# Entry of the up-projection: another order of the token halves Y, earlier places for split weights, and a written order for the stretch

## The chip, the cores and the metric

The kernel runs on one core of one Trainium2 chip. Its metric is the time in microseconds (us) of one execution on the device, as a median of three runs. TensorE (PE) does the matmuls, ScalarE (ACT) the activations, casts and copies, VectorE (DVE) most of the elementwise sums, GpSimd (POOL) a few products and the DMAs that accumulate; SyncE (SP) issues the other DMAs of this stretch. Each engine works through its own queue in order and waits on semaphores for the others.

## The reference, cut to what matters

One layer of an encoder in float32, with 512 tokens of 1024 channels. A mixing block (a gated recurrence beside attention) is followed by a feed-forward block. The change concerns the passage from the first to the second:

```python
h = rms_norm(x, ffn_norm_pre[layer])
up = jnp.einsum("bsd,df->bsf", h, w_up[layer])              # 1024 -> 6144
up = causal_dwconv(up, conv_f_w[layer], conv_f_b[layer])    # 3 taps over the tokens
gate, val = jnp.split(up, 2, axis=-1)
ffn_out = jnp.einsum("bsf,fd->bsd", jax.nn.gelu(gate) * val, w_down[layer])
x = x + rms_norm(ffn_out, ffn_norm_post[layer])
```

## The kernel before

**The split.** Every large product keeps float32 accuracy by splitting both sides into a high part (a cast) and a low part (what the cast lost). It takes three matmuls: high by high, high by low, low by high. The activations of the up-projection are `h2h` and `h2l`. The weights come as 48 tiles of 128 output channels, `up0` to `up47`. Tile `j` (gate) and tile `j + 24` (value) make pair `j`.

**Two kinds of tiles.** Pairs 0 to 2 are plain: their six tiles (`first` in the code: 0, 24, 1, 25, 2, 26) are split whole, and each is multiplied for token half X (`first_half`, tokens 0 to 255) and later for token half Y (tokens 256 to 511). One half is a `project_half` of 24 matmuls, 16 with the high weight and then 8 with the low one. Pairs 3 to 23 (class `Pair`) are done with a Strassen-like scheme, seven products in place of eight, each a `product` of 12 matmuls. The scheme needs:

- sums of activations over quarters, `sh` (ACT casts) and `sl`, made by `token_sums` from `hf`, one step for token tile 2 and one for token tile 3;
- plain pieces of raw weight tiles, `mh` (an ACT cast, `plain_high`) and `ml`: `plain_low` has ACT write the negative (L360), and POOL then issues a DMA that adds the raw weights to it (L361). For pair 3's first piece, DVE makes `ml`;
- sums of weights `t` (DVE, `sums`), with `th` (ACT cast, `sums_hi`) and `tl` (DVE, `sums_lo`). `th` and `tl` are taken from the same rotating buffers (tags `wh` and `wl`, four each) as the split weights of plain tiles 1, 25, 2 and 26;
- copies `x` of finished PSUM pieces (ACT, `keep`, L420) that DVE adds to others (`add`, L432).

**After a tile.** The convolution of a tile starts with one ACT instruction (`tap`, L1283) and goes on with two DVE instructions (`taps`, L1289), which read PSUM. For a pair there follow a gelu on ACT (L1293), a product `yf` on POOL (L1297) and a store to `yd`. For the plain pairs these steps are `first_tap`, `first_taps` and `first_glu`.

**What sets the order.** Up to the Y halves a scheduler arranges the instructions, from the code order and its own costs. From `man2` on (`manual_schedule`) each engine's queue has the order of the code. There `p` and `n` are pairs 3 and 4, the entry is written out by hand, and then the function `period` repeats for each pair: product 5 of the current pair, its sums, product 6, product 4 of the pair before, product 3, products 1 and 2 of the next pair, and product 7. In the entry PE goes through the Y halves and pair 3's products 1, 2 and 5, and then through the periods. `up_epilogue` says at which step of a period the tap, taps, gelu and GLU product of the pair before are done; in the first period, which has no pair before, its step 3 does the GLU of plain pairs 1 and 2.

**Where things lie.** The tiles `u` and `xn` of the norm (`mix_norm`) are in pool `norm`, as `hf` is. The pools `strassen` and `strassen1`, which hold `mh` and `ml`, are opened after the block `mix` is closed, that is behind the Y halves.

Of the kernel before, what the change touches and what calls it, by code (L numbers as in the profile page):

```python
# [63 lines left out]
def kernel(  # L64
# [162 lines left out]
    def project_half(dst, unit, ah, al, c):  # L227
        wh, wl = unit
        for k in range(KD):
            pe.matmul(dst[:, c], wh[:, k], ah[:, k, c], start=k == 0, stop=False)  # L230
            pe.matmul(dst[:, c], wh[:, k], al[:, k, c], start=False, stop=False)  # L231
        for k in range(KD):
            pe.matmul(dst[:, c], wl[:, k], ah[:, k, c], start=False, stop=k == KD - 1)
# [106 lines left out]
    class Pair:  # L340
# [36 lines left out]
                self.w[3] = quarter(h, l, A)  # L377

        def plain(self, i):
            self.plain_low(i)  # L380
            self.plain_high(i)

        def sums(self, i):
            r0, r1 = self.r
# [762 lines left out]
    def up_pair(j):  # L1147
        return Pair(ups, j, (f"up{j}", f"up{j + JF}"))

    turned = {}  # L1150
    with ExitStack() as mix:
# [2 lines left out]
        special["up0"] = special[f"up{JF}"] = wfpool  # L1154
        hf = npool.tile([P, KD, S], F32, name="hf", bufs=1)
        gb = [npool.tile([P, D], F32, name=f"gain{i}", bufs=1) for i in range(2)]
        for i in range(2):
            nc.sync.dma_start(gb[i], gains[i + 1 : i + 2, :].partition_broadcast(P))

        def mix_norm(t, acc):  # L1160
            u = npool.tile([P, D], F32, tag="u", name=f"u{t}")
            xn = npool.tile([P, D], F32, tag="xn", name=f"xn2_{t}")
            s2 = small.tile([P, 2], F32, tag="s2", name=f"s2_mix{t}")
            for i, c in enumerate(HALVES):
                act.activation(out=xn[:, c], in_=acc[t][i], func=AF.Square, accum_out=s2[:, i : i + 1])
                dve.tensor_tensor(out=u[:, c], in0=acc[t][i], in1=gb[0][:, c], op=ALU.mult)
            yield
            ss = small.tile([P, 1], F32, tag="ss", name=f"ss_mix{t}")
            dve.tensor_tensor(out=ss, in0=s2[:, 0:1], in1=s2[:, 1:2], op=ALU.add)
            rs = rstd_of(ss, f"mix{t}")  # L1170
            if t > 1:
                yield
            s3 = small.tile([P, 2], F32, tag="s2", name=f"s2_f{t}")
            for i, c in enumerate(HALVES):
                dve.scalar_tensor_tensor(out=x2t[:, t, c], in0=u[:, c], scalar=rs, in1=x2t[:, t, c],
                                         op0=ALU.mult, op1=ALU.add)
                act.activation(out=xn[:, c], in_=x2t[:, t, c], func=AF.Square, accum_out=s3[:, i : i + 1])
            yield
            ss = small.tile([P, 1], F32, tag="ss", name=f"ss_f{t}")
            dve.tensor_tensor(out=ss, in0=s3[:, 0:1], in1=s3[:, 1:2], op=ALU.add)  # L1180
            rs = rstd_of(ss, f"f{t}")
            for c in HALVES:
                dve.scalar_tensor_tensor(out=xn[:, c], in0=x2t[:, t, c], scalar=rs, in1=gb[1][:, c],
                                         op0=ALU.mult, op1=ALU.mult)
            yield
            turned[t] = to_channels(xn, t, h2h, h2l, hf, "f")
# [29 lines left out]
        def token_sums(t):  # L1216

            c1, c2 = (slice(P * (t - 2 + d), P * (t - 1 + d)) for d in (0, 2))
            f11, f12 = hf[:, :KH, c1], hf[:, KH:, c1]
            f21, f22 = hf[:, :KH, c2], hf[:, KH:, c2]  # L1220
            dve.tensor_tensor(out=f22, in0=f21, in1=f22, op=ALU.add)
            dve.tensor_tensor(out=f21, in0=f11, in1=f21, op=ALU.subtract)
            dve.tensor_tensor(out=f11, in0=f22, in1=f11, op=ALU.subtract)
            dve.tensor_tensor(out=f12, in0=f12, in1=f11, op=ALU.subtract)
            yield
            for i, f in enumerate((f22, f11, f21, f12)):
                act.copy(sh[i][:, :, c1], f)
                dve.tensor_tensor(out=sl[i][:, :, c1], in0=f, in1=sh[i][:, :, c1].bitcast(F32), op=ALU.subtract)
# [3 lines left out]
        def first_half(e, ready_only=False):  # L1232
            first.append((bank(f"up{e}"), unit(f"up{e}", 0)))
            project_half(*first[-1], h2h, h2l, X)
# [21 lines left out]
        s2 = token_sums(2)  # L1256
        next(s2)
        first_half(2 + JF)
        with ExitStack() as later:
            for i in turned[NT - 1]:  # L1260
                later.enter_context(tc.issue_after(i.ins))
            pairs[NU].sums(0)
            pairs[NU].sums(1)
            pairs[NU + 1] = up_pair(NU + 1)
            next(s2, None)
            for _ in token_sums(3):
                pass
        for ps, u in first:
            project_half(ps, u, h2h, h2l, Y)

    ypool = fstk.enter_context(tc.tile_pool(name="ff", bufs=3, reuse_waits="tile"))
    ydram = ctx.enter_context(tc.tile_pool(name="ffd", bufs=1, space=bass.MemoryType.DRAM))
    yd = [ydram.tile([P, 2, S], F32, name=f"yd{j}") for j in range(JF // 2)]
    upool = ustk.enter_context(tc.tile_pool(name="up", bufs=3, reuse_waits="tile"))
    offset(ustk, 32, "right")
    st1pool = ustk.enter_context(tc.tile_pool(name="strassen1", bufs=2, side="right", reuse_waits="tile"))
    offset(ustk, 416, "right")
    ups.stpools = [ustk.enter_context(tc.tile_pool(name="strassen", bufs=2, side="right", reuse_waits="tile")), st1pool]
    ups.kpool = upool

    def tap(e, ps, tag):
# [18 lines left out]
    def up_epilogue(b, which, step):  # L1300
        if which == "a" and step > 1 and not b:
            if step == 3:
                first_glu(1)
                first_glu(2)
        elif b and step == 0:
            e, ps, tag = (b.j, b.a, "cg") if which == "a" else (b.j + JF, b.c, "cv")
            b.u = getattr(b, "u", {})
            b.u[which] = tap(e, ps, tag)
        elif b and step == 1:
            e, ps = (b.j, b.a) if which == "a" else (b.j + JF, b.c)  # L1310
            taps(e, ps, b.u[which])
        elif b and step == 2:
            gelu(b.u["a"])
        elif b:
            glu(b.j, b.u["a"], b.u["c"])
# [3 lines left out]
    def first_tap(j):  # L1319
        fe[j] = [tap(e, first[2 * j + i][0], t) for i, (e, t) in enumerate(((j, "cg"), (j + JF, "cv")))]  # L1320

    def first_taps(j):
        for i, e in enumerate((j, j + JF)):
            taps(e, first[2 * j + i][0], fe[j][i])

    def first_glu(j):
        gelu(fe[j][0])
        glu(j, *fe[j])
# [1 line left out]
    man2 = ExitStack()  # L1330
    man2.enter_context(tc.manual_schedule())
    p, n = pairs[NU], pairs[NU + 1]
    p.sums_hi(0)
    p.sums_lo(0)
    p.sums_hi(1)
    p.sums_lo(1)
    p.plain_high(0)
    p.plain(1)
    n.sums(0)
    first_tap(0)  # L1340
    n.sums(1)
    first_taps(0)
    first_tap(1)
    n.plain(0)
    p.p12()
    p.keep(2, p.a[:, Y])
    p.add(p.a[:, X], p.a[:, X], 2)
    pairs[NU + 2] = up_pair(NU + 2)
    p.p5()
    n.sums_hi(0)  # L1350
    n.sums_lo(0)
    p.keep(1, p.c[:, X])
    first_taps(1)
    first_tap(2)
    n.sums_hi(1)
    n.sums_lo(1)
    first_glu(0)
    first_taps(2)
    PRODUCTS = (1, 4, 5, 6, 7, 3, 2)
    WQ = {1: (0, 0), 2: (1, 0), 3: (1, 1), 4: 3, 5: 0, 6: 1, 7: 2}  # L1360
    STEPS = [(n, m) for n in PRODUCTS for m in range(NS)]
# [337 lines left out]
```

## Time and profile before

| what | value |
| --- | --- |
| median of three runs | 922.22 us (921.89 to 922.26) |
| profiled execution | 919.4 us |
| its span, first to last instruction | 917.6 us |
| granted clock of PE | 0.999 |
| PE busy | 905.7 us (99%) |
| DVE busy | 723.1 us (79%) |
| ACT busy | 597.9 us (65%) |
| POOL busy | 216.5 us (24%) |

The profiled execution takes 1.8 us beside its span. Times inside it count from the start of the span. The six X halves end near 576 us, the Y halves run to 592 us, pair 3's first product follows, and the periods then take some 9.6 us each. In a row of the timeline stand the start, the length, the engine, the line, the operation, what it writes and reads, a count, and in square brackets how long the engine idled just before and what released it. Tile names have no number there. In the tables of order below they have one: `up_6736` is one tile, `_3` in `ml_3_6708` is the pair.

### The profile page before, as it was taken

To read this page: it belongs to the slowest core of one execution; us is meant where nothing else is said; L and a number is where in the kernel's file an instruction comes from. 1 tells how busy PE (TensorE), PEld (TensorE's weight loads), DVE (VectorE), ACT (ScalarE), POOL (GpSimd) and SP (SyncE) were. 2 spreads that over 40 slices of the span, in tenths; PEclk is the share of its full clock that TensorE was granted. 3 is DMA by queue.
4 is the path that set the end of the run, shared out by engine and by line. 5 is a ranking of instruction groups with operands and counts; after the bars stand their busy time and mean duration, and the time that the engine had idled before them with its cause. 6 is when DMAs were issued, how large, how long until landed. Compare 5 with 4: busy or idle time off the path is not lost.

```text
span 917.6 us, 15844 instructions
## 1 busy us (share of the span) xinstructions
PE 905.7 (99%) x5870; PEld 803.5 (88%) x5870; DVE 723.1 (79%) x1190; ACT 597.9 (65%) x1034; POOL 216.5 (24%) x279
## 2 busy tenths in 40 slices
PE   9999999999999999999999999999999999999997
PEld 7988888878899987888888889999999999978886
DVE  5966369638867657888868588899999999889897
ACT  7555495433467655676654487698888888676664
POOL 4134345444111112112104100042323223100000
PEclk9999999999999999999999999999999999999999
DMA  7777589989877776334415654289988988799764
GB/s 283 242 206 210 163 214 246 273 221 188 196 184 187 183 272 231 114 131 170 156 64 166 207 185 143 58 215 219 224 228 213 241 203 210 225 370 328 238 202 147
DMA packets 71760, 187.07 MB, mean 204 GB/s; under 512 B 7233, under 2 KB 27761, under 8 KB 71298
## 3 DMA queue, kind: packets, MB, share of 16 engines
q1 hardware_dynamic: 47648, 127.72, 41.6%
q0 software_dynamic: 23888, 58.20, 29.3%
q8 instruction: 46, 0.75, 0.3%
q14 instruction: 32, 0.26, 0.1%
q10 hardware_dynamic: 146, 0.14, 0.0%
HBM read 150.69 MB, written 35.73 MB: 203 GB/s over the span
## 4 chain that ended last, share of the span: by engine, by line
PE 94%; DMA 2%; DVE 2%; issue 1%; ACT 1%; POOL 0%; SPq 0%; DVEq 0%; ACTq 0%; POOLq 0%
PE up L416 7%; PE up L414 7%; PE up L413 7%; PE dn L1411 4%; PE dn L1409 4%; PE dn L1410 4%; PE pa L218 2%; PE ga L220 2%; PE ga L218 2%; PE pa L219 2%; PE pa L220 2%; PE ga L219 2%; PE q L218 2%; PE k L218 2%; PE pb L218 2%; PE wo L1141 2%
## 5 line engine op out<-in xcount | busy, mean ns | idle before, releaser
L1289 DVE SCALAR_TENSOR_TENSOR u<-up,cpt,u 128x511 f32<-128x511 f32 x96 | 71.2, 745 | 2.6 <-ACT u L1283 0.9
L361 POOL DMA_DIRECT2D ml<-raw_up x41 | 35.3, 862 | 153.6 <-ACT ml L360 78.8
L1409 PE MATMUL dn<-wh_dn,ah 128*128 128x512 f32 (+1 forms) x180 | 67.6, 376 | 0.7 <-ACT ah L1377 0.7
L1411 PE MATMUL dn<-wh_dn,al 128*128 128x512 f32 (+1 forms) x180 | 67.7, 376 | 0.0
L1410 PE MATMUL dn<-wl_dn,ah 128*128 128x512 f32 (+1 forms) x180 | 67.6, 375 | 0.0
L413 PE MATMUL up<-sh,th 128*128 128x256 f32 x252 | 60.3, 276 | 0.4 <-DVE up L432 0.4
L414 PE MATMUL up<-sl,th 128*128 128x256 f32 x252 | 60.2, 276 | 0.0
L175 DVE TENSOR_TENSOR wl_dn<-raw_dn,wh_dn 128x1024 fp32r<-128x1024 f32 x42 | 51.5, 1227 | 8.6 <-ACT wh_dn L172 8.4
L172 ACT CAST wh_dn<-raw_dn 128x1024 fp32r<-128x1024 f32 x42 | 44.1, 1050 | 18.2 <-issue 11.5
L325 DVE TENSOR_TENSOR tl<-t,th 128x1024 fp32r<-128x1024 f32 x42 | 51.1, 1216 | 2.8 <-ACT th L395 2.8
L1283 ACT ACTIVATE u<-up,cpt 128x512 f32<-128x512 f32 x48 | 37.0, 779 | 20.4 <-PE up L416 11.1
L413 PEld LDWEIGHTS up<-sh,th 128*128 128x128 f32 x252 | 47.3, 188 | 0.6 <-DVE up L432 0.6
L395 ACT CAST th<-t 128x1024 fp32r<-128x1024 f32 x42 | 43.9, 1044 | 5.5 <-PE up L231 2.1
L414 PEld LDWEIGHTS up<-sl,th 128*128 128x128 f32 x252 | 47.3, 188 | 0.0
L1297 POOL TENSOR_TENSOR yf<-u,u 128x512 f32<-128x512 f32 x23 | 30.6, 1333 | 63.5 <-issue 43.9
L413 PE MATMUL up<-h2h,mh 128*128 128x256 f32 x168 | 40.2, 276 | 0.0
L414 PE MATMUL up<-h2l,mh 128*128 128x256 f32 x168 | 40.2, 276 | 0.0
L1409 PEld LDWEIGHTS dn<-wh_dn,ah 128*128 128x128 f32 x180 | 33.9, 188 | 7.1 <-ACT ah L1377 1.1
L1411 PEld LDWEIGHTS dn<-wh_dn,al 128*128 128x128 f32 x180 | 33.9, 188 | 7.0 <-DVE al L325 0.8
L1410 PEld LDWEIGHTS dn<-wl_dn,ah 128*128 128x128 f32 x180 | 33.9, 188 | 6.0
L416 PE MATMUL up<-sh,tl 128*128 128x256 f32 x252 | 38.8, 276 | 0.0
L1000 ACT ACTIVATE P<-P,mx 128x384 f32<-128x384 f32 (+2 forms) x64 | 35.2, 552 | 3.7 <-DVE mx L995 2.8
(719 smaller groups left out, 3219.3 us busy)
## 6 DMA issues: line engine op xcount, KB each, us to landing
raw_up<-in_w_up_dram SPq DMA_DIRECT2D x48, 512.0 KB, 5.2
td<-in_w_down_dram POOLq DMA_DIRECT2D x36, 512.0 KB, 6.7
raw_dn<-td SPq DMA_DIRECT2D x24, 512.0 KB, 5.0
B<-cnd POOLq DMA_DIRECT2D x16, 640.0 KB, 5.5
ml<-raw_up POOLq DMA_DIRECT2D x20, 512.0 KB, 5.8
raw_dn<-in_w_down_dram SPq DMA_DIRECT2D x18, 512.0 KB, 4.5
raw_wo<-in_w_out_dram SPq DMA_DIRECT2D x16, 512.0 KB, 4.3
td<-td POOLq DMA_DIRECT2D x12, 512.0 KB, 13.2
```

The source lines that it names most:

```text
L172: act.copy(self.wh, self.raw)
L175: engine.tensor_tensor(out=self.wl, in0=self.raw, in1=self.wh.bitcast(F32), op=ALU.subtract)
L218: pe.matmul(dst, ah, bh, start=first, stop=False)
L325: dve.tensor_tensor(out=out, in0=a, in1=b, op=ALU.subtract)
L395: act.copy(self.th[i], self.t[i])
L413: pe.matmul(dst, wh[:, k], ah[:, k], start=first and k == 0, stop=False, skip_group_check=True)
L414: pe.matmul(dst, wh[:, k], al[:, k], start=False, stop=False, skip_group_check=True)
L416: pe.matmul(dst, wl[:, k], ah[:, k], start=False, stop=k == KH - 1, skip_group_check=True)
L1289: dve.scalar_tensor_tensor(out=c[:, s:], in0=ps[:, : S - s], scalar=col(C_CFW + 3 * e + j), in1=c[:, s:], op0=ALU.mult, op1=ALU.add)
L1409: pe.matmul(d[:, x], ah[:, k, tok], wh[:, k, x], start=first, stop=False, skip_group_check=True)
L1410: pe.matmul(d[:, x], ah[:, k, tok], wl[:, k, x], start=False, stop=False, skip_group_check=True)
L1411: pe.matmul(d[:, x], al[:, k, tok], wh[:, k, x], start=False, stop=last, skip_group_check=True)
```

## The change

It does four things.

1. `plain(i)` does nothing if the piece is there already.
2. `u` and `xn` get a pool of their own, `norm2`, which is closed after the last X half. The pools for `mh` and `ml` are opened there, so these can be written during the Y halves.
3. The stretch behind `p.sums` is put under `manual_schedule`. Pair 3's plain pieces are made at its start, the first step of `token_sums(3)` follows, the Y halves go in the order 1, 25, 2, 26, 0, 24, and the first `th` and `tl` of pair 3 and the rest of `token_sums(3)` come behind them in the code.
4. The written entry of `man2` is put in another order. Pair 4's weight sums and pieces come earlier; plain pairs 1 and 2 are tapped before plain pair 0. `first_taps` can do one tile of a pair. In step 3 of the first period stand now the taps of tile 24 and the GLU of plain pairs 2 and 0.

```diff
         def plain(self, i):
-            self.plain_low(i)
-            self.plain_high(i)
+            if i not in self.ml:
+                self.plain_low(i)
+                self.plain_high(i)
...
+        nstk = ExitStack()
+        n2pool = nstk.enter_context(tc.tile_pool(name="norm2", bufs=2, reuse_waits="tile"))
...
-            u = npool.tile([P, D], F32, tag="u", name=f"u{t}")
-            xn = npool.tile([P, D], F32, tag="xn", name=f"xn2_{t}")
+            u = n2pool.tile([P, D], F32, tag="u", name=f"u{t}")
+            xn = n2pool.tile([P, D], F32, tag="xn", name=f"xn2_{t}")
...
         first_half(2 + JF)
+        nstk.close()
+        offset(ustk, 32, "right")
+        st1pool = ustk.enter_context(tc.tile_pool(name="strassen1", bufs=2, side="right", reuse_waits="tile"))
+        offset(ustk, 416, "right")
+        ups.stpools = [ustk.enter_context(tc.tile_pool(name="strassen", bufs=2, side="right", reuse_waits="tile")), st1pool]
         with ExitStack() as later:
...
             pairs[NU + 1] = up_pair(NU + 1)
+        with tc.manual_schedule():
             next(s2, None)
-            for _ in token_sums(3):
-                pass
-        for ps, u in first:
-            project_half(ps, u, h2h, h2l, Y)
+            p.plain_high(0)
+            p.plain(1)
+            s3 = token_sums(3)
+            next(s3)
+            for ps, u in first[2:] + first[:2]:
+                project_half(ps, u, h2h, h2l, Y)
+            p.sums_hi(0)
+            p.sums_lo(0)
+            next(s3, None)
...
             if step == 3:
-                first_glu(1)
+                first_taps(0, 1)
                 first_glu(2)
+                first_glu(0)
...
-    def first_taps(j):
-        for i, e in enumerate((j, j + JF)):
-            taps(e, first[2 * j + i][0], fe[j][i])
+    def first_taps(j, *which):
+        for i in which or (0, 1):
+            taps(j + JF * i, first[2 * j + i][0], fe[j][i])
...
-    p.sums_hi(0)
-    p.sums_lo(0)
     p.sums_hi(1)
     p.sums_lo(1)
-    p.plain_high(0)
-    p.plain(1)
+    n.plain(0)
     n.sums(0)
-    first_tap(0)
     n.sums(1)
-    first_taps(0)
     first_tap(1)
-    n.plain(0)
+    first_taps(1)
+    first_tap(2)
     p.p12()
+    n.sums_hi(0)
+    n.sums_hi(1)
+    n.plain(1)
     p.keep(2, p.a[:, Y])
     p.add(p.a[:, X], p.a[:, X], 2)
     pairs[NU + 2] = up_pair(NU + 2)
     p.p5()
-    n.sums_hi(0)
     n.sums_lo(0)
     p.keep(1, p.c[:, X])
-    first_taps(1)
-    first_tap(2)
-    n.sums_hi(1)
     n.sums_lo(1)
-    first_glu(0)
+    first_glu(1)
+    first_tap(0)
     first_taps(2)
+    first_taps(0, 0)
```

Three places show what this does to the queues. The first is ACT's, from the first copy of pair 3 (`x_3`) to the first copy of pair 4 (`x_4`). `u_` are tiles of the convolution, `up_6222` and `up_6247` are plain tiles 0 and 24, `up_6430` and `up_6459` plain tiles 2 and 26. Before:

```order
L420 COPY x_3_6785<-up_6768 128x256
L1283 ACTIVATE u_6791<-up_6430,cpt 128x512
L1283 ACTIVATE u_6793<-up_6459,cpt 128x512
L395 CAST th_4_6795<-t_4_6720 128x1024
L1293 ACT_TABLE_LOAD
L1293 ACTIVATE u_6716<-u_6716 128x512
L420 COPY x_3_6819<-up_6736 128x256
L360 ACTIVATE ml_4_6821<-raw_up_6491 128x512
L369 CAST mh_4_6824<-raw_up_6491 128x512
L360 ACTIVATE ml_5_6826<-raw_up_6764 128x1024
L369 CAST mh_5_6841<-raw_up_6764 128x1024
L420 COPY x_4_6868<-up_6843 128x256
```

And after, where `up_6225` and `up_6250` are plain tiles 0 and 24, and the gelu is that of plain pair 1:

```order
L421 COPY x_3_6799<-up_6784 128x256
L1304 ACT_TABLE_LOAD
L1304 ACTIVATE u_6731<-u_6731 128x512
L1294 ACTIVATE u_6807<-up_6225,cpt 128x512
L1294 ACTIVATE u_6809<-up_6250,cpt 128x512
L421 COPY x_3_6829<-up_6743 128x256
L360 ACTIVATE ml_5_6831<-raw_up_6780 128x1024
L369 CAST mh_5_6846<-raw_up_6780 128x1024
L421 COPY x_4_6873<-up_6848 128x256
```

The second `th` of pair 4 and the `ml` and `mh` of its second tile have gone from between the copies; they stand ahead of pair 3's first copy.

The second place is DVE's queue from pair 3's first add to the steps `t` of pair 5. Before (the two taps `L1289` of each tile read `up_6300` and `up_6371`, plain tiles 1 and 25, then `up_6430` and `up_6459`):

```order
L325 TENSOR_TENSOR tl_4_6783<-t_4_6713,th_4_6781 128x1024
L1289 SCALAR_TENSOR_TENSOR u_6727<-up_6300,cpt,u_6727 128x511
L1289 SCALAR_TENSOR_TENSOR u_6727<-up_6300,cpt,u_6727 128x510
L1289 SCALAR_TENSOR_TENSOR u_6729<-up_6371,cpt,u_6729 128x511
L1289 SCALAR_TENSOR_TENSOR u_6729<-up_6371,cpt,u_6729 128x510
L325 TENSOR_TENSOR tl_4_6797<-t_4_6720,th_4_6795 128x1024
L1289 SCALAR_TENSOR_TENSOR u_6791<-up_6430,cpt,u_6791 128x511
L1289 SCALAR_TENSOR_TENSOR u_6791<-up_6430,cpt,u_6791 128x510
L1289 SCALAR_TENSOR_TENSOR u_6793<-up_6459,cpt,u_6793 128x511
L1289 SCALAR_TENSOR_TENSOR u_6793<-up_6459,cpt,u_6793 128x510
L432 TENSOR_TENSOR up_6843<-up_6843,x_4_6868 128x256
L432 TENSOR_TENSOR up_6768<-up_6736,x_3_6785 128x256
```

And after (`up_6433` and `up_6462` are plain tiles 2 and 26):

```order
L325 TENSOR_TENSOR tl_4_6801<-t_4_6728,th_4_6770 128x1024
L1300 SCALAR_TENSOR_TENSOR u_6739<-up_6433,cpt,u_6739 128x511
L1300 SCALAR_TENSOR_TENSOR u_6739<-up_6433,cpt,u_6739 128x510
L1300 SCALAR_TENSOR_TENSOR u_6741<-up_6462,cpt,u_6741 128x511
L1300 SCALAR_TENSOR_TENSOR u_6741<-up_6462,cpt,u_6741 128x510
L1300 SCALAR_TENSOR_TENSOR u_6807<-up_6225,cpt,u_6807 128x511
L1300 SCALAR_TENSOR_TENSOR u_6807<-up_6225,cpt,u_6807 128x510
L433 TENSOR_TENSOR up_6848<-up_6848,x_4_6873 128x256
L1300 SCALAR_TENSOR_TENSOR u_6809<-up_6250,cpt,u_6809 128x511
L1300 SCALAR_TENSOR_TENSOR u_6809<-up_6250,cpt,u_6809 128x510
L433 TENSOR_TENSOR up_6784<-up_6743,x_3_6799 128x256
L433 TENSOR_TENSOR up_6784<-up_6784,x_3_6829 128x256
```

The other `tl` of pair 4 stands just ahead of this piece. Between pair 3's add and pair 4's add there are two `tl` and six taps where there were two `tl` and eight taps, and two taps now follow pair 4's add.

The third place is POOL's queue, from the DMA for pair 3's second tile on. Before, with the GLU products `yf` of plain pairs 0, 1 and 2 in this order:

```order
L361 DMA ml_3_6708<-raw_up_6427 128x512
L361 DMA ml_4_6731<-raw_up_6490 128x1024
L1297 TENSOR_TENSOR yf_6800<-u_6716,u_6718 128x512
L361 DMA ml_4_6821<-raw_up_6491 128x512
L361 DMA ml_5_6826<-raw_up_6764 128x1024
L1297 TENSOR_TENSOR yf_6876<-u_6727,u_6729 128x512
L1297 TENSOR_TENSOR yf_6880<-u_6791,u_6793 128x512
L361 DMA ml_5_6910<-raw_up_6765 128x512
```

And after, with the GLU products of plain pairs 1, 2 and 0:

```order
L361 DMA ml_3_6526<-raw_up_6430 128x512
L361 DMA ml_4_6720<-raw_up_6508 128x1024
L361 DMA ml_4_6772<-raw_up_6509 128x512
L1308 TENSOR_TENSOR yf_6804<-u_6731,u_6733 128x512
L361 DMA ml_5_6831<-raw_up_6780 128x1024
L1308 TENSOR_TENSOR yf_6883<-u_6739,u_6741 128x512
L1308 TENSOR_TENSOR yf_6887<-u_6807,u_6809 128x512
L361 DMA ml_5_6917<-raw_up_6781 128x512
```

The DMA for pair 4's second tile has moved ahead of the first GLU product; the rest keeps its sequence, with other pairs in the three products.

More of the change, by code (lines that the diff above doesn't have):

```diff
@@ L1261 @@
                 later.enter_context(tc.issue_after(i.ins))
[L1262 to L1263 removed]
+            p = pairs[NU]
+            p.sums(0)
+            p.sums(1)
             pairs[NU + 1] = up_pair(NU + 1)
+        with tc.manual_schedule():
             next(s2, None)
[L1266 to L1269 removed]
+            p.plain_high(0)
[7 more added lines that the diff above has]
+            next(s3, None)
     ypool = fstk.enter_context(tc.tile_pool(name="ff", bufs=3, reuse_waits="tile"))
@@ L1274 @@
     upool = ustk.enter_context(tc.tile_pool(name="up", bufs=3, reuse_waits="tile"))
[L1275 to L1278, printed above, removed]
     ups.kpool = upool
```

## The prediction

> **What bounds the kernel now.** I read first the busy times on the page, then TensorE's waits, then, around the one pair of waits that the change can touch, the timelines of four engines.
>
> ```profile
> PE 905.7 (99%) x5870; PEld 803.5 (88%) x5870; DVE 723.1 (79%) x1190; ACT 597.9 (65%) x1034; POOL 216.5 (24%) x279
> ...
> PE up L416 <- DMA ml<-raw_up: 0.9, 1, 0.9
> ...
> PE dn L1409 <- ACT ah L1377: 0.7, 1, 0.7
> ...
> PE up L413 <- DVE up L432: 0.4, 1, 0.4
> ```
>
> TensorE (PE) is busy 99% of the span. It sets the time, and the change leaves its instructions as they are: only a stall of PE can be won or made. The list of its waits (engine, line, waited for: total, times, longest) has two in the up-projection, one for an `ml` of a pair and one for a sum of VectorE (DVE). The rest lie before and after the stretch that is edited; one of them, 0.7 in the down-projection, is shown. What the two cost is read from PE's timeline, since a wait also holds the pipelined matmuls behind it (columns: start, length, operation; an L416 row is the last third of one `product`):
>
> ```profile
> 595.40 0.62 PE L416 MATMUL up<-sh,tl 128*128 128x256 f32 x4
> ...
> 600.88 0.62 PE L416 MATMUL up<-h2h,ml 128*128 128x256 f32 x4
> 602.24 0.62 PE L416 MATMUL up<-sh,tl 128*128 128x256 f32 x4
> 603.60 0.62 PE L416 MATMUL up<-sh,tl 128*128 128x256 f32 x4
> ...
> 605.67 0.62 PE L416 MATMUL up<-sh,tl 128*128 128x256 f32 x4
> ...
> 608.42 0.64 PE L416 MATMUL up<-sh,ml 128*128 128x256 f32 x4
> 610.87 0.74 PE L416 MATMUL up<-h2h,ml 128*128 128x256 f32 x4 [0.89 <-DMA ml<-raw_up]
> 612.35 0.62 PE L416 MATMUL up<-h2h,ml 128*128 128x256 f32 x4
> ...
> 616.43 0.62 PE L416 MATMUL up<-sh,tl 128*128 128x256 f32 x4
> ```
>
> An undisturbed product takes 1.36 us (602.24 to 603.60). Stall 1: the last third of pair 4's product 6 starts at 605.67, 2.07 after the one before, so 0.71 is lost; it waits for pair 4's first add. Stall 2: from 608.42 over pair 5's product 1 to its product 2 at 612.35 are 3.93 for two products of 2.72, so 1.21 is lost; it waits for the `ml` of pair 5's first raw tile. Together 1.92 us, and nothing else in the stretch is PE's loss. The first places to look are the engines that came late:
>
> ```profile
> 594.69 0.37 ACT L420 COPY x<-up 128x256 f32<-128x256 f32 x1 [1.46 <-PE up L416]
> ...
> 596.05 0.37 ACT L420 COPY x<-up 128x256 f32<-128x256 f32 x1
> 596.32 1.45 ACT L1283 ACTIVATE u<-up,cpt 128x512 f32<-128x512 f32 x2
> 597.66 1.05 ACT L395 CAST th<-t 128x1024 fp32r<-128x1024 f32 x1
> ...
> 600.82 0.63 ACT L360 ACTIVATE ml<-raw_up 128x512 fp32r<-128x512 f32 x1
> ...
> 601.86 1.06 ACT L360 ACTIVATE ml<-raw_up 128x1024 fp32r<-128x1024 f32 x1
> ...
> 603.76 0.37 ACT L420 COPY x<-up 128x256 f32<-128x256 f32 x1
> 596.05 1.23 DVE L325 TENSOR_TENSOR tl<-t,th 128x1024 fp32r<-128x1024 f32 x1 [0.52 <-ACT th L395]
> ...
> 601.21 2.97 DVE L1289 SCALAR_TENSOR_TENSOR u<-up,cpt,u 128x511 f32<-128x511 f32 x4
> 604.16 1.23 DVE L432 TENSOR_TENSOR up<-up,x 128x256 f32<-128x256 f32 x3
> ```
>
> Stall 1 has two causes that end together. ScalarE (ACT) makes the copy `x` at 603.76 to 604.13, though the product that it copies was out at 601.50 (600.88 and 0.62). DVE ends its four taps at 604.18 and only then adds. Either alone, taken away, would leave the other. Stall 2 is read from the chain of waits (start, length, what):
>
> ```profile
> 600.75 1.03 POOL yf L1297
> ...
> 603.22 7.61 DMA ml<-raw_up
> ```
>
> GpSimd (POOL) issues pair 5's accumulating DMA at 603.22, behind ACT's `ml` of 601.86, a GLU product and the DMA of pair 4's second tile; it lands 7.61 later.
>
> **The change, part by part.** *Order of the Y halves and of the entry.* The casts `th` need slots that the split weights of plain tiles 1, 25, 2 and 26 hold until their Y halves' high matmuls end:
>
> ```profile
> 577.27 1.07 PE L233 MATMUL up<-h2h,wl_up 128*128 128x256 f32 x8
> ...
> 585.43 1.07 PE L233 MATMUL up<-h2h,wl_up 128*128 128x256 f32 x8
> 578.69 1.29 ACT L1227 CAST sh<-hf 128x512 fp32r<-128x512 f32 x2 [4.03 <-DVE hf L1221]
> 580.67 0.62 ACT L1227 CAST sh<-hf 128x512 fp32r<-128x512 f32 x1 [0.69 <-DVE hf L1223]
> 581.88 0.62 ACT L1227 CAST sh<-hf 128x512 fp32r<-128x512 f32 x1 [0.58 <-DVE hf L1224]
> 582.90 1.05 ACT L395 CAST th<-t 128x1024 fp32r<-128x1024 f32 x1 [0.41 <-PE up L231]
> 585.62 1.05 ACT L395 CAST th<-t 128x1024 fp32r<-128x1024 f32 x1 [1.67 <-PE up L231]
> ```
>
> The first two rows are the low thirds of the first and the fourth Y half, two of four rows that stand 2.72 apart, each starting as its high part ends. Tiles 1 and 25 stand third and fourth now, with 582.71 and 585.43, and the two casts of pair 3 start right behind. First and second in the order, they are free at 577.27 and 579.99, 5.44 earlier, and the two slots for pair 4 at 582.71 and 585.43. PE does the same matmuls: 0 in itself. What the earlier casts free is room on ACT and DVE ahead of 594.69, where ACT now idles 1.46, so pair 4's two `th` and its second tile's `ml` and `mh` can stand ahead of the first copy.
>
> *ACT between the two copies.* Between 596.05 and 603.76 it loses the second `th` (1.05) and the `ml` and `mh` of 512 columns (600.82 to 601.86, 1.04): 2.09. The two taps that were there are replaced by those of plain pair 0, the gelu by that of pair 1: equal. The copy moves to 601.67, just after its product (601.50), and ends at 602.04.
>
> *DVE between the two adds.* It keeps two `tl`, and six of eight taps stand ahead of pair 4's add. Two taps of 0.74 (2.97 over 4) go behind, and the 0.52 wait for `th` goes with the earlier casts: 604.16 less 1.48 and 0.52 is 602.16. The add, a third of 1.23, ends at 602.57; PE wants it when product 5's last four matmuls are issued (a third of 1.36 after 603.60), at 604.05. Stall 1 goes with 1.5 us to spare: −0.71.
>
> *POOL and the DMA.* Pair 5's `ml` on ACT starts 2.09 earlier, at 599.77, and ends at 600.83. Only one GLU product stands ahead of the DMA on POOL. Its gelu is no longer behind two taps (596.32 to 597.66, 1.34) and the `th` (1.05), so from 600.75 it moves up by 2.39 to 598.36 and ends by 600.07, with the 1.71 of its row below. Issue at 600.87. PE, without stall 1, wants it at 608.42 and 1.36 less 0.71, at 609.07. With its own 7.61 it lands at 608.48.
>
> ```profile
> DMA to landing us min/median/max: 4.6/6.0/8.5
> 600.75 1.71 POOL L1297 TENSOR_TENSOR yf<-u,u 128x512 f32<-128x512 f32 x1 [7.27 <-ACT u L1293]
> ...
> 604.74 3.00 POOL L1297 TENSOR_TENSOR yf<-u,u 128x512 f32<-128x512 f32 x2 [0.59 <-ACT u L1293]
> 605.30 1.29 DVE L325 TENSOR_TENSOR t<-raw_up,raw_up 128x512 f32<-128x512 f32 x1
> 606.51 1.78 DVE L325 TENSOR_TENSOR t<-raw_up 128x512 f32<-128x512 f32 x1
> 608.21 1.52 DVE L1289 SCALAR_TENSOR_TENSOR u<-up,cpt,u 128x511 f32<-128x511 f32 x2
> ...
> 614.68 1.22 DVE L432 TENSOR_TENSOR up<-up,x 128x256 f32<-128x256 f32 x3
> 615.81 0.68 DVE L325 TENSOR_TENSOR t<-raw_up,raw_up 128x512 f32<-128x512 f32 x1
> ```
>
> The first line holds the landings of these DMAs from 585 to 640: 4.6 to 8.5. At 8.5 it lands at 609.37 and 0.30 of stall 2 stays; at 7.61 or less it goes: −1.21, bound −0.91. I take the whole, since the DMA's own row is inside the spare time.
>
> *What is late next.* PE reaches pair 5's product 6 earlier by what was won. It starts now 8 matmuls ahead of its row at 616.43, which by 1.36 over 12 each is 615.52; with 1.92 won, 613.60. It waits for pair 5's add, now 614.68 to 615.09. DVE runs without a gap from 604.16 to there, so the add moves as DVE's work behind pair 4's add moves. Two taps go in there: 602.57 and 1.48 is 604.05 for the next adds, against 604.57 now, 0.5 earlier only. But the two `t` steps behind them take 2.91 now (605.30 to 608.21) against some 1.2 where nothing runs beside them (0.68 at 615.81, 0.60 from start to start). They coincide with two GLU products on POOL from 604.74 to 607.74. Of POOL's three GLU products, the first is done by 600.1 and the second starts 2.1 earlier, with its gelu. Only the third, held by its last tap to some 604.2 and 1.3 to 1.7 long (3.00 for two, at most 1.71 for one), meets the `t` steps, which start 0.5 earlier at 604.8. It holds them for 0.7 to 1.1 in place of 1.7. DVE is then 1.1 to 1.5 earlier, and the add ends at 613.6 to 614.0, when PE wants it at 613.60. Bounds: nothing given back, or 1.0 (a lead of 0.5 alone: the add ends at 614.6). I take the near end, 0 to 0.1, though the mean of 3.00 over two, 1.5, could leave 0.2.
>
> Opening the places of `mh` and `ml` sooner, and the skip in `plain`, cost 0: the casts of token tile 3 into `h2h` stand ahead of the first `mh` on ACT, and they need the last use of the room taken over. Were it held for longer, it would delay ACT, as in rival D.
>
> Sum against the profiled execution: 919.4 − 0.71 − 1.21 = 917.5. The median of the runs, 922.22, lies 2.8 above that execution; the difference carries over: **920.3 us**.
>
> **The rivals.** *(B) DVE gives it back.* If the gelus or GLU products are late by half a microsecond, both meet the two `t` steps as now, and PE waits at pair 5's product 6 for 0.3 to 1.0. For it: 605.30 and 606.51 take 1.29 and 1.78 against 0.68. Against it: the order of POOL. Gain 0.9 to 1.6, time 921.0. The Trainium skill ("SBUF — State Buffer", Who interferes with whom) says that a DVE instruction with two inputs in SBUF contends with a GpSimd instruction that reads SBUF, and that one with at most one such input does not. The trace agrees as far as it goes: the four taps at 601.21, with PSUM as one input, took 2.97 beside the product at 600.75. By that rule alone the whole of a GLU product can stand before a `t` step, which is the end of 1.0 here.
>
> *(C) The DMA stays late.* If it lands 8.5 after its issue, or the issue slips by a GLU product of 1.7 (order on POOL kept, gelu late), 0.3 to 1.2 of stall 2 stays. Against it: it is issued 2.4 earlier, ahead of the loads and stores that it met. Gain 0.7 to 1.6, time 921.1.
>
> *(D) Slower: the entry itself.* Four token-sum casts `sh`, which alternate with DVE's sums, then the second `th` of pair 3, six more casts and four taps now stand ahead of the first copy (594.69) on ACT in one fixed order. ACT's waits in the old entry (4.03, 0.69, 0.58, 0.41, 1.67) add up to 7.4. The last cast `sh` ends at 582.50 now. From there the list is five casts of 1.05, an `ml` and `mh` of 512 columns (1.04) and four taps at 0.67: 9.0, done by 591.5. PE wants the add behind that copy a third of a product after 595.40, at 595.85; the copy and the add take 0.8, so it must start by 595.0, and 3.5 are spare. If the fixed order brings 7.4 of waits again, all of them behind the last `sh`, PE stalls 3.9 at pair 3's product 6, against 1.92 won: +2.0, time 924.2. It is on the slow side from 5.4 late on. Against it: DVE's sums need nothing of PE, and 1.67 and 0.41 of the waits were for the slots that are free sooner now.
>
> *(E) Places held:* the plain casts cannot start sooner than before, and the order wins nothing: 922.2.
>
> **How the numbers follow.** Both waits go, with 0.1 at most given back: 0.56. B 0.16, C 0.14, D 0.12, E 0.02. A measurement of this kernel can tell some 0.2% (1.84 us) from no change. The forecast of 1.92 lies 0.08 beyond that, so 0.10 of its 0.56 falls within. Faster 0.46, same 0.42 (0.10, B, C, E), slower 0.12. The range: down by 1.92 and the 0.7 of the down-projection's wait, which shifted arrivals could also end, 919.6; up past the ends of B and C (921.3 and 921.5) toward E, to 922.0; D lies outside. The likeliest case's own range is 919.6 to 920.5.
>
> **What would show it.** Right: PE's waits have neither the row for `ml` nor that for L432; L416 rows are 1.36 apart from pair 4's product 6 to pair 5's product 6; the copy of pair 4 near 601.7, its add near 602.2, the DMA of pair 5 issued near 600.9. Wrong: a wait of PE for DVE's add at pair 5 (B), for an `ml` (C), or at pair 3's products 1 to 6 for `mh`, `tl` or the add (D).

## The result, and the profile after

The changed kernel is faster by about 0.15%. That is less than the forecast, and less than the 0.2% from which the prediction thought a gain could be told from none; with 22 runs of each, the interval of the ratio still leaves out 1.

| | before | changed |
| --- | --- | --- |
| median of 22 runs each | 920.85 us | 919.56 us |
| ratio to the kernel before, 95% interval | | 0.9985 (0.9979 to 0.9991) |
| second and third measurement, ratio | | 0.9986 (0.9977 to 0.9994), 0.9990 (0.9979 to 1.0001) |
| profiled execution, span | 919.4 us, 917.6 us | 919.7 us, 917.9 us |

The ratio stands for 1.4 us (0.8 to 1.9) where 1.92 was forecast. The two profiled executions don't show the gain in their spans, since they differ ahead of the stretch: the last Y half's low third starts at 590.87 before and at 592.17 after. Of these 1.30, 1.21 are there by the low third of the first X half (558.75 and 559.96), and 0.97 is one wait of PE near 12 us, in a part of the program that no edit touches. Over all the profiles of this study the start of the last low third lies between 590.87 and 594.31. So the stretch is measured here from that start to the start of the last third of pair 5's product 6, and this length is called L: 25.56 us before (616.43 less 590.87), 24.69 after, 23.64 without any stall. Times of the changed kernel less 1.30 compare with those of before.

PE's one wait in the stretch, and its timeline (columns as before; line numbers are one higher than before):

```profile
PE up L417 <- DMA ml<-raw_up: 0.7, 1, 0.7
...
603.55 0.62 PE L417 MATMUL up<-sh,tl 128*128 128x256 f32 x4
604.91 0.62 PE L417 MATMUL up<-sh,tl 128*128 128x256 f32 x4
606.27 0.62 PE L417 MATMUL up<-sh,tl 128*128 128x256 f32 x4
...
609.02 0.62 PE L417 MATMUL up<-sh,ml 128*128 128x256 f32 x4
611.29 0.74 PE L417 MATMUL up<-h2h,ml 128*128 128x256 f32 x4 [0.74 <-DMA ml<-raw_up]
612.78 0.62 PE L417 MATMUL up<-h2h,ml 128*128 128x256 f32 x4
...
616.86 0.62 PE L417 MATMUL up<-sh,tl 128*128 128x256 f32 x4
```

Stall 1 is gone: pair 4's product 6 (606.27) follows product 5 by 1.36. Stall 2 is there almost in full: 609.02 to 612.78 is 3.76 for two products of 2.72, so 1.04 in place of 1.21. The timelines of ACT, DVE, POOL and SyncE's queue (SPq) around it:

```profile
601.16 1.08 ACT L360 ACTIVATE ml<-raw_up 128x1024 fp32r<-128x1024 f32 x1
...
603.06 0.38 ACT L421 COPY x<-up 128x256 f32<-128x256 f32 x1
603.48 0.43 DVE L433 TENSOR_TENSOR up<-up,x 128x256 f32<-128x256 f32 x1
...
606.06 1.36 DVE L325 TENSOR_TENSOR t<-raw_up,raw_up 128x512 f32<-128x512 f32 x1
599.76 1.29 POOL L1308 TENSOR_TENSOR yf<-u,u 128x512 f32<-128x512 f32 x1 [6.64 <-DVE u L1300]
602.54 0.87 POOL L361 DMA_DIRECT2D ml<-raw_up  x1 [1.48 <-ACT ml L360]
...
605.57 1.30 POOL L1308 TENSOR_TENSOR yf<-u,u 128x512 f32<-128x512 f32 x1 [0.21 <-ACT mh L369]
601.08 0.33 SPq L1309 DMA_DIRECT2D yd<-yf  x1
601.58 1.47 SPq L347 DMA_DIRECT2D raw_up<-in_w_up_dram  x2
```

And the DMA's piece in the chain of waits (start, length):

```profile
602.54 8.71 DMA ml<-raw_up
```

Every engine was where the prediction had put it: less 1.30, the copy starts at 601.76 (601.67 forecast), the add at 602.18 (602.16), the `ml` at 599.86 (599.77). The DMA was issued at 601.24 (600.87 forecast) and took 8.71 to land where 7.61 was expected. SPq shows what is new beside it: both raw tiles of pair 6 are loaded in one go at 601.58. The second follows 1.1 later, 0.14 behind the DMA's issue. In the kernel before, by the same timeline, the first went out at 602.98 and the second 5 us later (the row spans both issues):

```profile
602.98 5.68 SPq L347 DMA_DIRECT2D raw_up<-in_w_up_dram  x2
```

### The profile page after: what moved, and what is told of

Read it like the earlier page. It is cut to its first block, busy times and chain, and to the rows that moved or that the text cites. A ratio compares the mean times of both kernels' runs of the same rounds, so it can differ in the third digit from the quotient of the medians.

```text
span 917.9 us, 15845 instructions
## 1 busy us (share of the span) xinstructions
PE 905.9 (99%) x5870; PEld 803.2 (88%) x5870; DVE 721.9 (79%) x1190; ACT 597.7 (65%) x1034; POOL 215.8 (24%) x279
## 4 chain that ended last, share of the span: by engine, by line
PE 89%; DMA 4%; DVE 4%; issue 1%; ACT 1%; POOL 0%; SPq 0%; DVEq 0%; ACTq 0%; POOLq 0%
PE up L417 7%; PE up L414 6%; PE up L415 6%; PE dn L1420 4%; PE dn L1418 4%; PE dn L1419 4%; DMA ml<-raw_up 2%; PE ga L218 2%; PE ga L219 2%; PE ga L220 2%; PE q L218 2%; PE k L218 2%; PE pb L218 2%; PE wo L1142 2%; PE k L220 2%; PE pb L219 2%
## 5 line engine op out<-in xcount | busy, mean ns | idle before, releaser
L433 DVE TENSOR_TENSOR up<-up,x 128x256 f32<-128x256 f32 x63 | 27.1, 432 | 13.8 <-PE up L417 9.4
```

## The experiments

Theory 1: the two loads of pair 6, issued just ahead of pair 5's accumulating DMA, hold it up. They go out together since the change makes pair 4's second piece early and so frees the raw tile that the second load needs (in the kernel before, SyncE waited 5.0 us there for pair 4's second DMA). The first load stands behind the store of the first GLU product in SyncE's queue, and so moved forward with that product. Theory 2: the DMA is slow in itself, by what POOL and DVE do beside it. L and the stalls of each run (the time of a product above 1.36 to 1.39, the usual ones; stall 2 over two products) are read from PE's timeline; landing is from issue to arrival of pair 5's first accumulating DMA.

| run | L | stall 1 | stall 2 | other stalls | landing | ratio (95%) |
| --- | --- | --- | --- | --- | --- | --- |
| before | 25.56 | 0.71 | 1.21 | | 7.6 | |
| changed | 24.69 | 0 | 1.04 | | 8.7 | 0.9985 (0.9979 to 0.9991) |
| changed, second | 25.05 | 0 | 1.13 | | 8.9 | 0.9986 (0.9977 to 0.9994) |
| changed, third | 24.30 | 0 | 0.65 | | 8.3 | 0.9990 (0.9979 to 1.0001) |
| load behind stores | 23.97 | 0 | 0 | | 5.5 | 0.9987 (0.9977 to 0.9996) |
| old, early piece | 24.44 | 0.66 | 0 | | 7.1 | 0.9980 (0.9971 to 0.9988) |
| piece put back | 24.78 | 0 | 0 | 0.70 at pair 5's product 6, 0.40 ahead | 6.7 | one run |
| old, loads behind stores | | 0.64 | 0 | pair 6 late on purpose | 5.4 | one run |
| old order of halves | 24.49 | 0 | 0 | 0.75 at pair 3's product 6, 0.09 at pair 5's | 5.5 | 0.9988 (0.9979 to 0.9997) |
| old, fewer taps | 25.74 | 0.72 | 0.46 | 0.63 before, 0.27 after | 7.5 | one run |
| pair 5's DMA first | 23.98 | 0 | 0 | 0.33 at pair 5's product 6 | 6.0 | 0.9989 (0.9978 to 1.0001) |
| and product onto pieces | 24.62 | 0 | 0 | 0.69 at pair 5's product 6 | 6.0 | 0.9995 (0.9984 to 1.0005) |
| and product onto taps | 23.92 | 0 | 0 | | 5.4 | 0.9977 (0.9967 to 0.9987) |
| the same, second | 23.65 | 0 | 0 | | 6.1 | 0.9977 (0.9966 to 0.9987) |

Each L and each landing is that of one execution. In five of them with an L (the second of the changed kernel, the load behind stores, the product onto pieces, the first of the product onto taps, and in part the old one with the early piece) some products take 1.41 for no wait that the trace shows; this adds 0.1 to 0.3 to L. The ratios are uncertain by 0.1%, about 0.9 us, so neighbours are compared by their stalls. That the end of stall 2 by itself shortens the whole program is not shown by them: in the two runs that only take it off the changed kernel (load behind stores, pair 5's DMA first) they are 0.9987 and 0.9989.

**The load alone.** Pair 6's second load moves behind two stores on SyncE:

```diff
-            for r, e in zip(self.r, tiles):
+            for r, e in zip(self.r[:1] if tiles[0] == "up6" else self.r, tiles):
...
                 first_glu(0)
+                late = pairs[NU + 3]
+                nc.sync.dma_start(late.r[1], ups.block(late.tiles[1]))
```

> The changed kernel, with one edit: the load of pair 6's second raw tile is issued behind the stores of plain pairs 2 and 0, not right behind the load of its first tile. L is the time from the start of the last Y half's low third to the last third of pair 5's product 6: 25.56 before, 24.69 after the change, 23.64 without any stall. Theory 1 (the two loads of pair 6 now go out together just ahead of pair 5's accumulating DMA and hold it up): that DMA lands in 7.6 or less in place of 8.7, the stall at pair 5's product 1 falls from 1.04 to 0.5 or less, L is 23.7 to 24.2, time 0.5 to 1.0 below the changed kernel. Theory 2 (the DMA is slow in itself, by POOL and the elementwise work beside it): landing stays at 8.3 or more, L 24.5 to 24.8, time as the changed kernel.

Landing 5.5, stall 2 gone, L 23.97, of which 0.3 is slow products. Nothing on ACT, DVE or POOL was changed. So theory 2 falls: POOL's row and DVE's steps were the same, and the DMA took 3.2 us less. The time agrees less well: a ratio of 0.9987 shows no gain over the changed kernel, though its interval has room for it. POOL's and SPq's timelines of this run:

```profile
604.13 0.87 POOL L361 DMA_DIRECT2D ml<-raw_up  x1 [1.49 <-ACT ml L360]
603.17 0.69 SPq L347 DMA_DIRECT2D raw_up<-in_w_up_dram  x1
...
608.92 0.42 SPq L1318 DMA_DIRECT2D raw_up<-in_w_up_dram  x1
```

**The kernel before, with pair 4's second piece early.**

```diff
     n.plain(0)
+    n.plain(1)
     p.p12()
```

(and `plain` skips a piece that is there, as in the change.)

> The kernel before, with one edit: the plain piece of pair 4's second tile (ml, mh and the accumulating DMA) is made ahead of pair 3's products 1 and 2, as in the changed kernel. It takes 1.04 of ACT from between the two copies and frees the raw tile early. Theory 1: DVE is still late, so the stall at pair 4's product 6 stays at 0.6 to 0.7; pair 6's two loads now go out together here too, pair 5's DMA is issued about 1 us sooner but lands 8.3 or more later, and the stall at pair 5's product 1 is 0.7 to 1.2: L 25.0 to 25.6, time within 0.5 of the kernel before. Theory 2: the DMA lands in 7.6 as before, the second stall falls to 0.3 or less, L 24.3 to 24.8. If ACT alone was the cause of the first stall, it goes too and L falls by a further 0.7.

Stall 1 stayed at 0.66 as expected. The loads did go out together, but the DMA landed in 7.1, not in 8.3 or more, and stall 2 was gone. By its numbers this run came out as theory 2 had it (L 24.3 to 24.8), and it is the load moved alone that speaks against theory 2. The timelines of POOL and SPq show what differs from the changed kernel:

```profile
603.71 0.85 POOL L361 DMA_DIRECT2D ml<-raw_up  x1
604.29 0.83 SPq L347 DMA_DIRECT2D raw_up<-in_w_up_dram  x2
```

Here the first load follows the DMA's issue by 0.58; in the changed kernel it stands ahead of it by 0.96. Theory 1 has to be narrower: two loads cost much more when the first is ahead of the DMA. Behind it they still cost something, 7.1 against 5.4 to 6.1 in the runs that have no load near. This one edit took 1.12 off L, more than the whole change's 0.87, and its ratio is among the lowest.

**The piece put back** in the changed kernel (the line `n.plain(1)` taken out of the entry, so that `period` makes the piece):

> The changed kernel with the plain piece of pair 4's second tile put back behind pair 3's products (all else as changed). Theory 1: the raw tile is free late again, so pair 6's second load goes out 5 us later than its first, and pair 5's DMA meets only one load and pair 4's second DMA: landing 5.5 to 7.6, issue about 1 us later than in the changed kernel, the stall at pair 5's product 1 0.3 to 1.0; the copy of pair 4 is 1.04 later, but the add still in time; L 24.0 to 24.7. Theory 2: landing 8.3 or more on the later issue, stall 1.5 to 2.1, L 25.2 to 25.8.

L is 0.08 above theory 1's range, and by another way. The second load goes out 5 us later again, the DMA lands in 6.7 as expected, and stall 2 is gone, where 0.3 to 1.0 was expected. But pair 4's add now waits for ACT's late copy, all of DVE behind it is 1 us later, and the add for pair 5 makes PE wait (DVE's timeline of this run):

```profile
604.49 0.43 DVE L433 TENSOR_TENSOR up<-up,x 128x256 f32<-128x256 f32 x1 [1.08 <-ACT x L421]
...
615.43 1.23 DVE L433 TENSOR_TENSOR up<-up,x 128x256 f32<-128x256 f32 x3
```

**The kernel before, with both loads of pair 6 behind the stores** (the loads of `Pair.__init__` for this pair moved behind `first_glu(2)` in step 3):

> The kernel before with one edit: both loads of pair 6 are issued behind the stores of plain pairs 1 and 2, so that none runs beside pair 5's accumulating DMA. Theory 1 (the loads are what makes that DMA long): it lands in 4.6 to 6.0 in place of 7.6, and the stall at pair 5's product 1 falls from 1.21 to 0.3 or less; the first stall stays at 0.7; later pair 6 may come late, which this run makes on purpose. Theory 2: landing 7.3 or more, the second stall stays.

Landing 5.4 in place of 7.6 with pair 4's DMA still ahead of it, and pair 5's products 1 and 2 at 1.37 and 1.36. So it was the loads that made stall 2 in the kernel before, too, as far as one execution tells. That pair 6 then came late cost 3.4 us at one later wait, which this run was not about.

**The order of the Y halves.**

```diff
-            for ps, u in first[2:] + first[:2]:
+            for ps, u in first:
```

> The changed kernel with the order of the Y halves undone (0, 24, 1, 25, 2, 26); all else as changed. Theory 1 (the order is what gives ACT room, since the casts th wait for the slots): the list on ACT ends about 0.6 late for pair 3's first copy, a new wait for DVE's add at pair 3's product 6 of 0.4 to 1.0 appears, L 25.1 to 25.7. Rival: the spare time on ACT holds it, L 24.7, and the order of the halves is worth nothing by itself.

The new stall is where it was expected: 0.75 at pair 3's product 6. ACT's timeline of this run shows the end of its list, with the second `mh` of pair 4 done at 596.42, and the copy behind it instead of waiting for PE:

```profile
592.72 0.78 ACT L1294 ACTIVATE u<-up,cpt 128x512 f32<-128x512 f32 x1 [1.08 <-PE up L233]
593.40 1.98 ACT L396 CAST th<-t 128x1024 fp32r<-128x1024 f32 x2
...
596.32 0.84 ACT L421 COPY x<-up 128x256 f32<-128x256 f32 x2
```

The first row adds a reason that the prediction hadn't: the tap of tile 26 stands in ACT's list, and with that tile last in the order it waits 1.08 for its Y half. In this execution the DMA landed in 5.5, between two loads issued over 2 us apart (the first of which took 8.4), so stall 2 was gone, and L, at 24.49, came out below both forecasts and below the changed kernel's. The order of the halves by itself is worth the 0.75 of the new stall; in this execution the stall that went was worth more.

**The kernel before, with two taps fewer ahead of the add** (those of tile 26 moved behind it):

> The kernel before with one edit: the two taps of plain tile 26 go behind pair 4's first add on DVE. DVE is then free 1.48 sooner, ACT is as before. If both engines were late together, the copy of ACT holds the add and the stall at pair 4's product 6 stays at 0.6 to 0.75, L 25.3 to 25.6. If DVE alone was the cause, the stall goes, L 24.8 to 24.9.

DVE was free and the stall stayed at 0.72, held by ACT's copy, as DVE's row for the add shows:

```profile
605.14 0.43 DVE L432 TENSOR_TENSOR up<-up,x 128x256 f32<-128x256 f32 x1 [1.42 <-ACT x L420]
```

Together with the run of the early piece, where ACT was relieved and DVE was not, this shows that stall 1 had two causes, each enough alone. L is 0.14 above the range: the next adds are two taps later, and pair 3's product 4 waits for them (1.77).

**Pair 5's DMA first.** In the changed kernel, ACT makes this `ml` ahead of the gelu table:

```diff
     n.sums_lo(1)
+    pairs[NU + 2].plain_low(0)
     first_glu(1)
```

(and `period` skips it where it is there.)

> The changed kernel with one edit: ACT makes the ml of pair 5's first tile right behind its second copy of pair 3, ahead of the gelu table, and POOL issues its accumulating DMA ahead of the first GLU product, some 3 us sooner. Theory 1 and theory 2 alike: it lands by 606 to 608 in this kernel's times, the stall at pair 5's product 1 goes, L 23.64 to 23.9, time 0.9 to 1.05 below the changed kernel. Rival (VectorE then is the limit at pair 5's product 6): a wait of PE for DVE's add there of 0.3 to 1.0, L 24.0 to 24.7.

Issued at 597.96, it landed in 6.0, and stall 2 is gone. The rival came true in part: 0.33 at pair 5's product 6. The ratio, 0.9989, doesn't show the gain that was expected. PE's, DVE's and POOL's timelines of this run, where PE's rows are the last thirds of pair 5's products 5 and 6:

```profile
613.44 0.62 PE L417 MATMUL up<-sh,tl 128*128 128x256 f32 x4
615.13 0.64 PE L417 MATMUL up<-sh,tl 128*128 128x256 f32 x4
605.05 1.56 DVE L325 TENSOR_TENSOR t<-raw_up,raw_up 128x512 f32<-128x512 f32 x1
...
613.61 1.22 DVE L433 TENSOR_TENSOR up<-up,x 128x256 f32<-128x256 f32 x3
604.77 1.29 POOL L1309 TENSOR_TENSOR yf<-u,u 128x512 f32<-128x512 f32 x1 [0.42 <-DVE up L433]
```

**The GLU product moved, twice.** The aim is to free the step `t`. In one run the gelu and the GLU product of plain pair 0 are moved behind pair 5's second piece; in another only the product is moved, to behind pair 6's first DMA. Both have pair 5's DMA first.

```diff
                 first_glu(2)
-                first_glu(0)
+                gelu(fe[0][0])
...
         elif b and step == 1:
+            if b.j == NU and which == "a":
+                glu(0, *fe[0])
```

(This is the second; the first calls `first_glu(0)` at step 0 of the next pair's value tile.)

> The changed kernel with two edits: pair 5's first DMA ahead of the first GLU product (as in the run before it), and the gelu and GLU product of plain pair 0 moved behind pair 5's second piece, into the next period, so that on POOL it falls on DVE's taps, not on its steps t. Theory 1 (of VectorE: with the DMA early, the 0.33 left at pair 5's product 6 comes from the first step t, 1.56 in place of 0.68, held by the GLU product beside it): that step takes 0.68 to 0.75, DVE's add for pair 5 is 0.7 to 0.9 sooner, no stall stays between pair 3's product 1 and pair 5's product 6, L 23.64 to 23.8 (with products at 1.36), time 1.0 to 1.3 below the changed kernel. Rival (the step is slow by its own, or the next GLU product takes the place): the step stays above 1.2, L 23.95 or more.

It fell on the step again, just ahead of it, and made it longer: 2.00, with 0.69 lost at pair 5's product 6. Pair 6's first DMA then landed in 10.1 and cost 1.5 over pair 6's products 1 and 2, which the expectation didn't foresee; the ratio, 0.9995, is the worst of the table.

> The changed kernel with pair 5's first DMA ahead of the first GLU product, and with only the GLU product of plain pair 0 moved (its gelu stays): on POOL it stands behind pair 6's first DMA, so it falls on DVE's taps and last tl. Theory (a GLU product that runs when a step t is next holds that step for its whole length): the first step t of pair 5 takes 0.68 to 0.8, where it took 1.36 in the changed kernel, 1.56 with the DMA early and 2.00 with the product begun just ahead of it; the add for pair 5 is 0.5 to 0.9 sooner; no stall from pair 3's product 1 to pair 5's product 6, L 23.64 to 23.8 (products at 1.36), time 0.9 to 1.3 below the changed kernel and 1.7 to 2.2 below the kernel before. Rival (the steps are slow by their own, or the product costs the last tl as much): L 23.95 or more.

DVE's and POOL's timelines of this run:

```profile
607.23 0.68 DVE L325 TENSOR_TENSOR t<-raw_up,raw_up 128x512 f32<-128x512 f32 x1
607.83 0.68 DVE L325 TENSOR_TENSOR t<-raw_up 128x512 f32<-128x512 f32 x1
612.37 1.64 POOL L1309 TENSOR_TENSOR yf<-u,u 128x512 f32<-128x512 f32 x1
```

Both steps take 0.68, the product runs on the taps, and PE has no wait in the stretch. The second measurement, with no slow product, gives L at 23.65, 1.91 below before:

> The same kernel as in the run with the product moved onto the taps, once more, beside the changed kernel on one chip. No stall between pair 3's product 1 and pair 5's product 6 (L 23.64, plus at most 0.4 where products take 1.41); the first step t 0.68; time 0.5 to 1.3 below the changed kernel, ratio to the kernel before 0.9975 to 0.9985.

> The changed kernel a third time, as the measure for the other: landing of pair 5's first DMA 8.5 to 9, the stall at pair 5's product 1 1.0 to 1.2; ratio to the kernel before 0.998 to 0.999.

Twice 0.9977, 2.1 us below the kernel before. The changed kernel beside it had 0.9990 (medians of 919.41 and 920.63 us on the same chip). So this version has the lowest ratio of the study and no stall in the stretch; its interval still overlaps with that of the changed kernel, and with that of the old kernel with the early piece (0.9980). The second run of the changed kernel was to tell whether stall 2 was chance:

> The changed kernel once more, beside the others on this chip. If the stall at pair 5's product 1 is a feature of the order: landing 8 to 9, L 24.5 to 24.9. If it was chance in one execution: landing 5.5 to 7.6, L 23.9 to 24.3. Time 0.9 to 1.9 below the kernel before either way.

Stall 2 was 1.13 with a landing of 8.9, and 0.65 with one of 8.3 in the third run, below what was expected there. It is there each time, in size between 0.65 and 1.13.

## Why the prediction was right and wrong

- **Stall 1: right.** Forecast −0.71, measured −0.71, with the copy within 0.1 us and the add within 0.02 of the forecast. That either engine alone would leave it was shown by two runs.
- **The DMA of stall 2: wrong, and the term that was mis-sized.** Forecast −1.21, measured −0.17 (−0.08 and −0.56 in the other two profiles). The step that failed is "the DMA's own row is inside the spare time". It landed 8.71 after its issue (8.9 and 8.3 in the other two), and the issue was 0.37 late; of the 1.47 that this makes, 0.59 was spare, which left 0.88, and PE lost 1.04. The landing of 7.61 belonged to the traffic of before, with one load near it and pair 4's DMA ahead of it. Rival C even had it "ahead of the loads and stores that it met", and that was the reverse of the truth. In the rows of before a load stood 0.24 ahead of it already. This load moved forward with the first GLU product, and the early piece of pair 4 freed a raw tile, so that the second load went out with it: one 0.96 ahead of the DMA's issue, the other within about 0.2 of it. The prediction followed each moved instruction and its own DMA, but not the store and the load behind a moved product, nor the buffer that a moved cast set free. A smaller part is the time from ACT's end to POOL's issue, 0.30 (602.24 to 602.54). It was in the rows of before (ACT's `ml` ends at 592.30, POOL starts at 592.60); the prediction counted 0.04, and the missing 0.26 is most of the 0.37 by which the issue was late.
- **What is late next: right in kind, short in size.** The add for pair 5 was said to end when PE wants it, with 0 to 0.1 given back and 0.4 at the far end of its times. Behind stall 2 it didn't show. With the DMA early it was 0.33.
- **The rivals.** C is what happened, by loads and not by POOL's order; its 0.7 to 1.6 holds the measured 1.4. B came out as the next limit. D did not occur: ACT idled 3.51 ahead of pair 3's first copy, against 3.5 spare forecast. It takes the old order of the halves to bring it near.
- **The number.** 919.56 lies 0.04 under the range, which is not the gain's doing, as that was smaller than forecast. The base was: the three runs shown had 922.22, 22 runs have 920.85. The 2.8 us between median and profiled execution, which the sum carried over, hold 1.4 by which these three runs lay above the median of 22. And the profiled execution had the earliest start of the stretch of all profiles of the study (590.87; the others 591.15 to 594.31).

The gain of the stalls in the profiles is 0.87 us for the first profile, 0.8 for the second with its slow products taken off (0.26 in six), 1.26 for the third; the ratios give 0.9 to 1.4. Whether there is more to find in the later part is not shown: the wait of 0.7 in the down-projection reads 0.2, 0.4 and 1.7 in the three profiles of the changed kernel, so it varies from one execution to the next.

## What to carry to other kernels

An instruction that moves earlier also frees its source earlier, and whatever waited for that buffer starts with it: follow the buffer to the transfer that takes it, and see which transfer that one now goes out beside. A landing time belongs to the traffic of its moment, and is no property of a DMA (the same 512 KB took from 5.4 to 8.9 here); give it a range from rows with other neighbours before it is set against a slack of 0.6 us. When a stall goes, the engine that was only just in time becomes the next one, and here it paid to move a product of a mostly idle engine away from the step that it held.

## What the runs showed of the hardware

**Two loads issued close to an accumulating DMA can hold back all of it.** The DMA view of the changed kernel for 604 to 606 (first row, the only queue in that window) and for 606 to 608, and that of the kernel before for 604 to 606 (packets, MB, share of the 16 engines; q1 holds SyncE's transfers, q0 those of POOL):

```profile
q1 hardware_dynamic: 154, 0.57, 104.6%
...
q1 hardware_dynamic: 107, 0.39, 76.5%
q0 software_dynamic: 21, 0.09, 21.5%
...
q1 hardware_dynamic: 53, 0.17, 60.9%
q0 software_dynamic: 63, 0.13, 41.8%
```

The changed kernel's DMA was issued at 602.54, and up to 607 its queue moved nothing while the two loads went; where the DMA went first and met no load, its first packets came 1.0 to 1.5 after the issue. With the first load 0.96 ahead and the second within about 0.2 of its issue it landed in 8.3 to 8.9, with the second load 4.8 behind in 5.5, with the two 0.58 and 1.0 behind in 7.1. The Trainium skill ("DMA: Bandwidth & Descriptors", Issuing engines are not separate DMA queues) says that DMAs from different issuers run on the same 16 engines and interleave. The kernel before agrees, with both queues moving in the same 2 us (POOL's with pair 4's DMA ahead of pair 5's); in the changed kernel there was no interleaving from the issue to 607. It can also go the other way round. In the run with the old order of the halves the first load was issued 0.87 ahead of the DMA, and from 604 to 606 only the DMA's queue moved; that load took 8.4 and the DMA 5.5. What decides which of the two goes first is not shown.

**A step `t` on DVE ends a fixed time after the GLU product that it meets.** It ended at 607.42 with the product's end at 606.87 in the changed kernel, at 606.61 with 606.06 where the DMA came first, and at 610.41 with 609.85 where the product was begun just ahead: 0.55 to 0.56 later each time, about its own 0.60 from start to start. That fits a step that does not run until the product is done, which is what the Trainium skill's rule on two inputs in SBUF, named in rival B, gives. The taps, which read PSUM, were not held: two of them took 1.53 beside the product of 1.64, and 1.53 with no product beside them.
